# Recurrence levels multiplied as 32x32 diagonal blocks in one core's hybrid decoder layer

## The chip, the cores and the metric

The kernel runs on one core of a Trainium2 chip. The metric is the device time of one execution in microseconds (us), lower being better. Matrix products run on TensorE (PE in the profile; its weight loads are PEld), elementwise work on VectorE (DVE), ScalarE (ACT) and GpSimd (POOL), and transfers are issued mostly from SyncE (SP).

## The reference

One decoder layer over 16 learned tokens ("meta") and 2048 sequence tokens of width 1024. An input projection feeds three token mixers; their outputs are joined, projected, normalised, and go through a gated MLP. The change is inside the second mixer, a gated linear recurrence of four heads of width 128, which the reference computes chunk by chunk:

```python
G = jnp.cumsum(gb, axis=2)                              # gb: log of the forget gate
diff = G[:, :, :, None, :] - G[:, :, None, :, :]
decay = jnp.where(mask, jnp.exp(jnp.where(mask, diff, 0.0)), 0.0)   # lower triangle
A = jnp.einsum('bhtd,bhsd,bhtsd->bhts', qb, kb, decay)
o_intra = jnp.einsum('bhts,bhse->bhte', A, ib)
```

Every pair of tokens s <= t has its own vector of decays, so A is not one product of two matrices.

## The kernel before

The sequence goes through the mixers in four blocks of 512 tokens (`NB`, `TB`), each held as four tiles of 128 tokens (`TT`, `P`). Block 0 also carries the 16 meta tokens. For each block `Mixers.run` is a generator that issues the big projections: `cols_proj` and `rows_proj` multiply activations by weights through `mm3` (L117 to L119), three products per operand pair, since each operand is split in a rounded part and a remainder (`split`, L112 on ACT and L113 on DVE, into `w_hi` and `w_lo`, three buffers of each).

For each block and head, `Mixers.head` builds the 128x128 matrix A of each of the four tiles by levels of doubling. At the level of run length w, tokens are paired in runs of w; the products of all keys of an even run with all queries of the odd run next to it can be written with one common reference point, and so become a matrix product. `level(w, ka, qa)` does this for w = 1 (before the loop over `LEVELS`; its mask also takes the diagonal) and, in the loop, for w = 2, 4, 8 and 16: 5 calls per head, 80 in all. Each call multiplies the whole 128x128 tile (L402, four matmuls into one bank), and one masked copy on DVE (L403, `copy_predicated`, 128x512) takes the valid entries into A. In block 0, calls with w < 16 (4 per head, 16 in all) also do the 16x16 matrix of the meta tokens (L407, L408). For w = 32 and 64, `level_wide` multiplies only the blocks that are needed (L415: eight matmuls with 32 weight columns for w = 32, in partitions 0-31 and 64-95 in turn; four with 64 for w = 64) and copies these blocks into A (L419). POOL and DVE prepare the operands of each level (L427, L428, L430, L431). At the end of the head A is the weight operand of L486.

The masks are built once at the start by `level_masks` on POOL: five 128x128 tiles, each with a buffer of its own.

What sets the order: `drive` interleaves the generators, one step of a head after each step of the projections; PE keeps exactly the order in which the program issues its instructions (`manual_schedule`), while the other engines' queues are ordered by a scheduler ahead of the run, from priorities (weight loads and splits are raised by `AHEAD`) and its own model of times.

Of the kernel before, what the change touches and what calls it, by code (L numbers as in the profile page):

```python
# [10 lines left out]
F32 = mybir.dt.float32  # L11
F32R = mybir.dt.float32r
U32 = mybir.dt.uint32
# [5 lines left out]
P = 128  # L19
# [7 lines left out]
TT = TB // P  # L27
# [5 lines left out]
T_CB, T_CC, T_CV, T_Q, T_F, T_PV = 0, 2, 4, 6, 10, 14  # L33
POOL_WINDOWS = (2, 4, 8, 16)
LEVELS = (2, 4, 8, 16, 32, 64)
ALPHA = 2.0 ** 0.25
LN_EPS = 1e-5
RMS_EPS = 1e-6
# [16 lines left out]
def bcast_rows(row, n):  # L55

    return bass.AP(row.tensor, row.offset, [[0, n], row.ap[-1]])


class Common:  # L60
# [38 lines left out]
    def bank(self):  # L99
        return self.ps.tile([P, 512], F32, tag="bank", name="bank")  # L100
# [115 lines left out]
class Mixers:  # L216
# [5 lines left out]
    def __init__(self, ctx, cm, lower, w_feat, w_rows, w_conv, w_pool, pool_scale, norm_g, w_o, x, xT, meta,  # L222
                 metaT, ln1, x1):
        self.cm, self.nc = cm, cm.nc
        nc, tc = cm.nc, cm.tc
        self.x, self.xT, self.meta, self.metaT, self.ln1, self.x1 = x, xT, meta, metaT, ln1, x1
        self.key_eng = nc.gpsimd
        self.pooled = []
        self.w_feat, self.w_rows, self.w_o = w_feat, w_rows, w_o
        cpool = ctx.enter_context(tc.tile_pool(name="m_const", bufs=1))  # L230
        self.ipool = ctx.enter_context(tc.tile_pool(name="m_i", bufs=5))
        self.hpool = ctx.enter_context(tc.tile_pool(name="m_h", bufs=1))

        self.ng = cpool.tile([P, P], F32, name="ng")
        nc.gpsimd.dma_start(self.ng, bcast_rows(norm_g, P))
        self.ctaps = cpool.tile([P, 2, 3], F32, name="ctaps")
        nc.gpsimd.dma_start(self.ctaps, w_conv)
        self.pscale = cpool.tile([P, 2], F32, name="pscale")
        nc.gpsimd.dma_start(self.pscale, pool_scale)
        self.wp = cpool.tile([P, 2, P], F32, name="wp")  # L240
        nc.vector.memset(self.wp, 0.0)
        for m in range(2):
            for h in range(2):
                nc.gpsimd.dma_start(self.wp[h * 64:(h + 1) * 64, m, h * 64:(h + 1) * 64], w_pool[2 * m + h])
        self.lower_bounds(cpool, lower)
        self.level_masks(cpool)


        self.cnt = cpool.tile([P, 2, NM], F32, name="cnt")
        for m in range(2):  # L250
            nc.gpsimd.iota(self.cnt[:, m, :], pattern=[[1, NM]], base=1, channel_multiplier=0,
                           allow_small_or_imprecise_dtypes=True)
            for h in range(2):
                hs = slice(h * 64, (h + 1) * 64)
                nc.vector.tensor_scalar_min(self.cnt[hs, m, :], self.cnt[hs, m, :],
                                            float(POOL_WINDOWS[2 * m + h]))
        nc.vector.reciprocal(self.cnt, self.cnt)


        self.a_buf = [cpool.tile([P, TT, P], F32, name=f"a{i}") for i in range(2)]  # L260
        self.a_meta = cpool.tile([NM, NM], F32, name="a_meta")
        for t in self.a_buf + [self.a_meta]:
            nc.vector.memset(t, 0.0)

        self.inv = cpool.tile([P, WC], F32, name="inv")
        nc.vector.memset(self.inv, 1.0)
        self.state = [cpool.tile([P, P], F32, name=f"state{h}") for h in range(NH)]
        self.chalo = [cpool.tile([P, 2], F32, name=f"chalo{m}") for m in range(2)]
        self.phalo = [cpool.tile([P, NM], F32, name=f"phalo{m}") for m in range(2)]
# [23 lines left out]
    def level_masks(self, pool):  # L293

        nc = self.nc
        self.masks = {}
        for h in (1, 2, 4, 8, 16):
            mk = pool.tile([P, P], F32, name=f"mask{h}")
            nc.gpsimd.memset(mk, 1.0)
            a = P // (2 * h)  # L300
            if h > 1:

                v = mk.rearrange("p (a u s) -> p a u s", u=2, s=h)
                nc.gpsimd.memset(v[:, :, 0, :], 0.0)
                t, pat = v[:, :, 1, :], [[1, a], [0, h]]
                tests = [(ALU.is_ge, 0, -2 * h, 1), (ALU.is_gt, h, 2 * h, -1)]
                for op, base, step, sign in tests:
                    nc.gpsimd.affine_select(out=t, in_=t, compare_op=op, fill=0.0, base=base,
                                            pattern=[[step, a], [0, h]], channel_multiplier=sign)
            else:  # L310

                v = mk.rearrange("p (a u) -> p a u", u=2)
                tests = [(0, ALU.is_equal, 0, -2, 1), (1, ALU.is_ge, 0, -2, 1), (1, ALU.is_ge, 1, 2, -1)]
                for u, op, base, step, sign in tests:
                    nc.gpsimd.affine_select(out=v[:, :, u], in_=v[:, :, u], compare_op=op, fill=0.0, base=base,
                                            pattern=[[step, a]], channel_multiplier=sign)
            self.masks[h] = mk.bitcast(U32)

    def row_tiles(self, b):
        return [(NM + t * P, P) for t in range(TT)] + ([(0, NM)] if b == 0 else [])  # L320
# [51 lines left out]
    def head(self, b, h, q, k, pre, vals, gates, sums, outs):  # L372
# [6 lines left out]
        nc, cm, s, bank = self.nc, self.cm, self.span(b), self.cm.bank  # L379
        mm = nc.tensor.matmul  # L380

        def runs(t, w, sl):
            return t[:, sl].rearrange("p (a u s) -> p a u s", u=2, s=w)
# [9 lines left out]
        nc.vector.tensor_mul(prep[:, :, 1, :], prep[:, :, 1, :], prep[:, :, 0, :])  # L393
        yield 2

        A, Am = self.a_buf[h % 2], self.a_meta
        main = [NM + t * P for t in range(TT)]

        def level(w, ka, qa):
            pt = bank()  # L400
            for t, c in enumerate(main):
                mm(pt[:, t * P:(t + 1) * P], lhsT=ka[:, c:c + P], rhs=qa[:, c:c + P], start=True, stop=True)  # L402
            nc.vector.copy_predicated(A, self.masks[w].unsqueeze(1).to_broadcast([P, TT, P]),  # L403
                                      pt.rearrange("p (t c) -> p t c", t=TT))
            if b == 0 and w < NM:
                pm = bank()
                mm(pm[0:NM, 0:NM], lhsT=ka[:, 0:NM], rhs=qa[:, 0:NM], start=True, stop=True)  # L407
                nc.vector.copy_predicated(Am, self.masks[w][0:NM, 0:NM], pm[0:NM, 0:NM])  # L408

        def level_wide(w, M):  # L410
            pt = bank()
            starts = range(0, P, 2 * w)
            for t, c in enumerate(main):
                for o in starts:
                    mm(pt[o:o + w, t * P + o + w:t * P + o + 2 * w],  # L415
                       lhsT=M[:, c + o:c + o + w], rhs=M[:, c + o + w:c + o + 2 * w], start=True, stop=True)
            ptv = pt.rearrange("p (t c) -> p t c", t=TT)
            for o in starts:
                nc.vector.tensor_copy(A[o:o + w, :, o + w:o + 2 * w], ptv[o:o + w, :, o + w:o + 2 * w])  # L419

        level(1, kB, qB)
        for w in LEVELS:
            sl = slice(0 if b == 0 and w < NM else NM, WC)
            M = self.wide("work", WORK)
            Mv, kv, qv, prev, postv = (runs(t, w, sl) for t in (M, k, q, pre, post))
            end = [P, prev.shape[1], w]
            self.key_eng.tensor_mul(Mv[:, :, 0, :], kv[:, :, 0, :], postv[:, :, 0, :])  # L427
            self.key_eng.tensor_mul(postv[:, :, 0, :], postv[:, :, 0, :],  # L428
                                    prev[:, :, 1, w - 1:w].to_broadcast(end))
            nc.vector.tensor_mul(Mv[:, :, 1, :], qv[:, :, 1, :], prev[:, :, 1, :])  # L430
            nc.vector.tensor_mul(prev[:, :, 1, :], prev[:, :, 1, :], prev[:, :, 0, w - 1:w].to_broadcast(end))  # L431
            yield 1
            if w < 32:
                level(w, M, M)
            else:
                level_wide(w, M)
        qG, kG = self.wide("work", WORK), self.wide("work", WORK)
        self.key_eng.tensor_mul(kG[:, s], k[:, s], post[:, s])
        nc.vector.tensor_mul(qG[:, NM:], q[:, NM:], pre[:, NM:])
# [11 lines left out]
        pt = bank()  # L451
# [136 lines left out]
    def out_proj(self, b, half, res):  # L588
# [11 lines left out]
        for (u, c, n), r in zip(prod, res):  # L600
            nc.vector.scalar_tensor_tensor(r[0:n, nn], in0=r[0:n, nn], scalar=ALPHA, in1=u[0:n],
                                           op0=ALU.mult, op1=ALU.add)
# [86 lines left out]
class Ffn:  # L689
# [357 lines left out]
    def down(self, b):  # L1047
# [4 lines left out]
        for t in range(2 * nu):  # L1052
            r = self.dpool.tile([P, D], F32, tag="row", name="row", bufs=2 * nu + 2)
            t0 = b * UT + t * P
            nc.sync.dma_start(r, self.x1[NM + t0:NM + t0 + P, :])
            nc.scalar.mul(r, r, ALPHA)
            rows.append(r)
# [175 lines left out]
```

## Time and profile before

| | us |
|---|---|
| median of 3 runs | 2333.89 (2333.07 to 2335.82) |
| the profiled execution, its own time | 2332.45 |
| its span, first to last instruction | 2330.7 |
| PE busy in the span | 2249.5 (97%) |
| DVE busy | 1673.3 (72%) |
| ACT busy | 890.6 (38%) |
| POOL busy | 860.0 (37%) |
| mean granted TensorE clock | 0.988 of full speed |

The head work lies between about 50 and 881 us; the rest of the span is the MLP, which has no levels. A busy engine is one with an instruction in flight; matmuls overlap in the pipeline, so what one of them costs is read from the distance between starts, not from its duration. One fp32 matmul leaves two records in the trace (320 matmuls on L402 are 640 records), one in the rounded format of L117 to L119 leaves one.

### The profile page before, as it was taken

The numbers are of one execution on the slowest core, as the hardware profiler recorded it, in microseconds if no ns is written. First come the engines' busy times: TensorE is split into PE (matmuls) and PEld (weight loads), VectorE is DVE, ScalarE is ACT, GpSimd is POOL, SyncE is SP. The second block draws the span as 40 slices with busy tenths as digits, with TensorE's granted clock in tenths as the row PEclk, the third lists the DMA queues.
The fourth block names the chain that finished last, engine by engine and source line by source line (L and its number), as shares of the span: only waits on it lengthen the run. The fifth ranks groups of instructions, "written<-read, shape, count | busy, mean of one in ns | idle before, by whom it ended". The sixth has DMA issues, their size and how long they took to land.

```text
span 2330.7 us, 33935 instructions
## 1 busy us (share of the span) xinstructions
PE 2249.5 (97%) x12692; PEld 1923.7 (83%) x12692; DVE 1673.3 (72%) x2277; ACT 890.6 (38%) x1400; POOL 860.0 (37%) x872
## 2 busy tenths in 40 slices
PE   8999999999999999999998997999999999999996
PEld 6898878788878877899998997788888887887775
DVE  4676777777857697887787777777777756475658
ACT  3233322332343235344443445444444454344332
POOL 3442433143315236354367443444444414000400
PEclk9999999999999999999999998999999999999998
DMA  6222222422452254555566436566666586567553
GB/s 211 67 71 92 73 68 88 159 82 71 149 183 73 82 166 153 207 187 189 191 199 243 145 146 216 187 190 203 196 197 195 189 299 222 195 236 244 181 183 133
DMA packets 182536, 382.25 MB, mean 164 GB/s; under 512 B 16722, under 2 KB 78370, under 8 KB 182372
## 3 DMA queue, kind: packets, MB, share of 16 engines
q1 hardware_dynamic: 166692, 336.66, 43.6%
q10 hardware_dynamic: 14496, 40.06, 4.7%
q0 software_dynamic: 1184, 3.37, 0.4%
q8 instruction: 99, 1.62, 0.3%
q14 instruction: 65, 0.53, 0.1%
HBM read 275.63 MB, written 104.41 MB: 163 GB/s over the span
## 4 chain that ended last, share of the span: by engine, by line
PE 80%; DVE 7%; POOL 4%; DMA 4%; issue 3%; ACT 1%; SPq 0%; DVEq 0%; ACTq 0%; POOLq 0%
PE bank L895 32%; PE bank L1044 14%; PE bank L117 9%; PE bank L118 9%; PE bank L119 9%; PE bank L402 3%; DVE w_lo L113 2%; POOL pw L563 1%; ACT w_hi L112 1%; DMA row<-x 1%; DVE row L210 1%; PE bank L415 1%; PE bank L676 1%; DVE row L959 1%; PE bank L485 1%
## 5 line engine op out<-in xcount | busy, mean ns | idle before, releaser
L113 DVE TENSOR_TENSOR w_lo<-raw,w_hi 128x512 fp32r<-128x512 f32 (+1 forms) x467 | 483.4, 1052 | 289.0 <-ACT w_hi L112 282.1
L112 ACT CAST w_hi<-raw 128x512 fp32r<-128x512 f32 (+1 forms) x467 | 359.6, 787 | 794.8 <-PE bank L119 257.1
L1044 PE MATMUL bank<-w_hi,w_lo 128*128 128x512 f32 x616 | 242.3, 393 | 9.7 <-DVE w_lo L113 9.6
L1044 PE MATMUL bank<-w_hi 128*128 128x512 f32 x616 | 240.9, 391 | 4.1 <-ACT w_hi L112 4.1
L959 DVE SCALAR_TENSOR_TENSOR row<-row,f_taps 128x1024 f32<-128x1024 f32 x176 | 237.0, 1348 | 9.6 <-ACT row L956 4.5
L1044 PE MATMUL bank<-w_lo,w_hi 128*128 128x512 f32 x616 | 240.6, 391 | 0.0
L117 PE MATMUL bank<-xhi,w_hi 128*128 128x512 f32 (+1 forms) x640 | 235.5, 368 | 0.0
L119 PE MATMUL bank<-xhi,w_lo 128*128 128x512 f32 (+1 forms) x640 | 226.0, 353 | 0.1
L118 PE MATMUL bank<-xlo,w_hi 128*128 128x512 f32 (+1 forms) x640 | 226.0, 353 | 0.0
L112 ACT CAST w_hi<-s 128x1024 fp32r<-128x1024 f32 x88 | 92.4, 1051 | 310.6 <-PE bank L895 203.0
L113 DVE TENSOR_TENSOR w_lo<-s,w_hi 128x1024 fp32r<-128x1024 f32 x88 | 124.2, 1412 | 75.0 <-ACT w_hi L112 74.2
L1044 PEld LDWEIGHTS bank<-w_hi,w_lo 128*128 128x128 f32 x616 | 116.0, 188 | 40.0 <-DVE w_lo L113 16.2
L956 ACT ACTIVATE row<-row,f_bias,f_taps 128x1024 f32<-128x1024 f32 x88 | 109.6, 1246 | 78.7 <-DVE row L950 74.9
L1044 PEld LDWEIGHTS bank<-w_hi 128*128 128x128 f32 x616 | 116.2, 189 | 28.1 <-ACT w_hi L112 4.6
L1077 POOL TENSOR_TENSOR row<-row,du 128x512 f32<-128x512 f32 x24 | 47.6, 2017 | 248.3 <-DVE du L1075 246.5
L1044 PEld LDWEIGHTS bank<-w_lo,w_hi 128*128 128x128 f32 x616 | 116.1, 189 | 25.0
L119 PEld LDWEIGHTS bank<-xhi,w_lo 128*128 128x128 f32 x640 | 121.0, 189 | 17.7 <-DVE w_lo L113 0.5
L117 PEld LDWEIGHTS bank<-xhi,w_hi 128*128 128x128 f32 x640 | 121.2, 189 | 16.6 <-ACT chi L112 0.5
L118 PEld LDWEIGHTS bank<-xlo,w_hi 128*128 128x128 f32 x640 | 121.4, 190 | 15.2 <-issue 0.7
L117 PE MATMUL bank<-w_hi,xhi 128*128 128x512 f32 x272 | 112.9, 415 | 7.6 <-ACT xhi L112 7.6
L428 POOL TENSOR_TENSOR work<-work,pre 128x256 f32<-128x256 f32 (+1 forms) x96 | 88.1, 917 | 82.0 <-DVE pre L431 61.5
L117 PE MATMUL bank<-w_hi,chi 128*128 128x512 f32 x272 | 112.1, 412 | 2.8 <-ACT w_hi L112 2.8
(293 smaller groups left out, 5601.2 us busy)
## 6 DMA issues: line engine op xcount, KB each, us to landing
raw<-a_ops SPq DMA_DIRECT2D x70, 512.0 KB, 4.6
raw<-in_w_up_dram SPq DMA_DIRECT2D x66, 512.0 KB, 4.9
raw<-in_w_feat_dram SPq DMA_DIRECT2D x64, 512.0 KB, 3.3
s_up<-s SPq DMA_DIRECT2D x44, 512.0 KB, 2.7
a_ops<-a_t SPq DMA_DIRECT2D x88, 256.0 KB, 2.1
s<-s_up SPq DMA_DIRECT2D x44, 512.0 KB, 5.2
raw<-s_down SPq DMA_DIRECT2D x40, 512.0 KB, 3.6
a_ops<-row SPq DMA_DIRECT2D x66, 256.0 KB, 2.5
```

The lines of the kernel that those rows point to most:

```text
L112: self.nc.scalar.copy(hi, src)
L113: self.nc.vector.tensor_sub(lo, src, hi.bitcast(F32))
L117: mm(out, lhsT=a_hi, rhs=b_hi, start=first, stop=False)
L118: mm(out, lhsT=a_hi, rhs=b_lo, start=False, stop=False)
L119: mm(out, lhsT=a_lo, rhs=b_hi, start=False, stop=last)
L402: mm(pt[:, t * P:(t + 1) * P], lhsT=ka[:, c:c + P], rhs=qa[:, c:c + P], start=True, stop=True)
L428: self.key_eng.tensor_mul(postv[:, :, 0, :], postv[:, :, 0, :], prev[:, :, 1, w - 1:w].to_broadcast(end))
L895: mm(u[:, 0:n], lhsT=wp[:, kc], rhs=xp[o][k][:, at:at + n], start=start, stop=k == 3 and i == 2, skip_group_check=True)
L956: nc.scalar.activation(y, c[:, 2:UT + 2], AF.Identity, bias=self.bias[:, i:i + 1], scale=self.taps[:, i, 2:3])
L959: nc.vector.scalar_tensor_tensor(y, in0=c[:, d:UT + d], scalar=self.taps[:, i, d:d + 1], in1=y, op0=ALU.mult, op1=ALU.add)
L1044: mm(bank, lhsT=x, rhs=y, start=first and k == 0 and i == 0, stop=k == HK - 1 and i == 2, skip_group_check=True)
L1077: nc.gpsimd.tensor_add(rows[t][:, f], rows[t][:, f], us[u])
```

## The change

`level` multiplies, for each tile, only the four 32x32 blocks on the diagonal: sixteen matmuls with 32 weight columns and 32 moving columns instead of four with 128 and 128. Block o of a tile goes to partitions o to o+31 of the bank, tile t to columns 32t to 32t+31, so the four blocks lie side by side. The masked copy then covers 128x128 elements and goes into a tile of its own, `near` (two of them, taken in turn by heads). After all levels of a head, four ACT copies of 32x(4x32) move `near` into the diagonal blocks of A. The masks become 128x32: each full mask is built in one of two buffers in turn and its four diagonal blocks are copied by ACT.

```diff
+R = 32
-        for t in self.a_buf + [self.a_meta]:
+        self.near = [cpool.tile([P, TT, R], F32, name=f"near{i}") for i in range(2)]
+        for t in self.a_buf + self.near + [self.a_meta]:
             nc.vector.memset(t, 0.0)
...
-            mk = pool.tile([P, P], F32, name=f"mask{h}")
+            mk = pool.tile([P, P], F32, tag="mask", name="mask", bufs=2)
...
-            self.masks[h] = mk.bitcast(U32)
+            near = pool.tile([P, R], F32, name=f"mask{h}")
+            for o in range(0, P, R):
+                nc.scalar.copy(near[o:o + R], mk[o:o + R, o:o + R])
+            self.masks[h] = near.bitcast(U32)
...
-        A, Am = self.a_buf[h % 2], self.a_meta
+        A, Am, near = self.a_buf[h % 2], self.a_meta, self.near[h % 2]
...
             for t, c in enumerate(main):
-                mm(pt[:, t * P:(t + 1) * P], lhsT=ka[:, c:c + P], rhs=qa[:, c:c + P], start=True, stop=True)
-            nc.vector.copy_predicated(A, self.masks[w].unsqueeze(1).to_broadcast([P, TT, P]),
-                                      pt.rearrange("p (t c) -> p t c", t=TT))
+                for o in range(0, P, R):
+                    mm(pt[o:o + R, t * R:(t + 1) * R], lhsT=ka[:, c + o:c + o + R], rhs=qa[:, c + o:c + o + R],
+                       start=True, stop=True)
+            nc.vector.copy_predicated(near, self.masks[w].unsqueeze(1).to_broadcast([P, TT, R]),
+                                      pt[:, 0:TT * R].rearrange("p (t c) -> p t c", t=TT))
...
+        for o in range(0, P, R):
+            nc.scalar.copy(A[o:o + R, :, o:o + R], near[o:o + R])
```

On PE nothing changes place; here is the last `level` call of block 0, head 0, before, between the input projection's matmuls (w_hi, xhi are split operands, work the level's operand).

```order
L117 MATMUL bank<-w_hi,xhi_117 16x512
L118 MATMUL bank<-w_lo,xhi_117 16x512
L119 MATMUL bank<-w_hi,xlo_125 16x512
L402 MATMUL bank<-work 128x128 x4
L117 MATMUL bank<-w_hi,xhi_118 128x512
L118 MATMUL bank<-w_lo,xhi_118 128x512
```

And now, at the same place.

```order
L118 MATMUL bank<-w_hi,xhi_117 16x512
L119 MATMUL bank<-w_lo,xhi_117 16x512
L120 MATMUL bank<-w_hi,xlo_125 16x512
L410 MATMUL bank<-work 32x32 x16
L118 MATMUL bank<-w_hi,xhi_118 128x512
L119 MATMUL bank<-w_lo,xhi_118 128x512
```

The four matmuls became sixteen small ones, and the projection goes on behind them as before. ACT's queue gets new entries; before, at the end of block 0, head 3, it read so (a weight split is a CAST, kT and km belong to the head's next steps).

```order
L176 DMA row<-in_xT_dram 128x1024
L112 CAST w_hi<-raw 128x512 x5
L450 COPY km<-bank 16x128
L455 COPY kT<-bank 128x512
L112 CAST w_hi<-raw 128x512
```

Now the four copies of `near` into A stand between two weight splits.

```order
L177 DMA row<-in_xT_dram 128x1024
L113 CAST w_hi<-raw 128x512 x2
L447 COPY a_223<-near_226 32x4x32 x4
L113 CAST w_hi<-raw 128x512 x3
L461 COPY km<-bank 16x128
L466 COPY kT<-bank 128x512
```

Three weight splits are queued behind the copies there. The other fifteen heads get their four copies at the corresponding place, some with an ACT operation of another part of the block between them.

## Rows read from the trace of the kernel before

**Rows 1.** The page's first line, and one stretch by engine (--windows).

```profile
PE 2249.5 (97%) x12692; PEld 1923.7 (83%) x12692; DVE 1673.3 (72%) x2277; ACT 890.6 (38%) x1400; POOL 860.0 (37%) x872
60.00:870.00 810.00, 801.15 (x4642) 667.61 (x4639) 596.15 (x1032) 263.18 (x571) 284.83 (x290) 1.00 0.31 101
```

**Rows 2.** PE's waits, 0 to 900 us: total us, times, longest.

```profile
PE bank L117 <- ACT xhi L112: 7.6, 1, 7.6
PE bank L485 <- DVE st L468: 6.6, 4, 2.4
```

**Rows 3.** PE's timeline at a level without meta: start, us, operation.

```profile
269.22 0.40 PE L118 MATMUL bank<-w_lo,xhi 128*128 128x512 f32 x1
269.45 0.39 PE L119 MATMUL bank<-w_hi,xlo 128*128 128x512 f32 x1
269.69 1.05 PE L402 MATMUL bank<-work 128*128 128x128 f32 x8
270.50 0.48 PE L117 MATMUL bank<-xhi,w_hi 128*128 128x512 f32 x1
270.81 0.39 PE L118 MATMUL bank<-xlo,w_hi 128*128 128x512 f32 x1
```

**Rows 4.** PE's timeline at a level with meta, block 0.

```profile
70.11 0.39 PE L119 MATMUL bank<-w_hi,xlo 128*16 128x512 f32 x1
70.34 1.05 PE L402 MATMUL bank<-work 128*128 128x128 f32 x8
71.32 0.21 PE L407 MATMUL bank<-work 128*16 128x16 f32 x2
...
71.80 0.40 PE L118 MATMUL bank<-w_lo,xhi 128*128 128x512 f32 x1
```

**Rows 5.** PE's timeline at a w = 32 level (L415).

```profile
284.23 0.39 PE L119 MATMUL bank<-xhi,w_lo 128*128 128x512 f32 x1
284.55 0.45 PE L415 MATMUL bank<-work 128*32 128x32 f32 x16
284.92 0.50 PE L117 MATMUL bank<-w_hi,chi 128*128 128x512 f32 x1
285.26 0.40 PE L118 MATMUL bank<-w_lo,chi 128*128 128x512 f32 x1
```

**Rows 6.** Another w = 32 level, from two later starts: first record left, records left.

```profile
84.34 0.39 PE L415 MATMUL bank<-work 128*32 128x32 f32 x14
...
84.46 0.27 PE L415 MATMUL bank<-work 128*32 128x32 f32 x6
```

**Rows 7.** PE by line and form: records, busy us, mean ns.

```profile
L402 PE MATMUL bank<-work 128*128 128x128 f32 x640 | 84.3, 275 | 0.1
L415 PE MATMUL bank<-work 128*64 128x64 f32 x128 | 10.9, 228 | 0.0
L415 PE MATMUL bank<-work 128*32 128x32 f32 x256 | 7.1, 199 | 0.0
```

**Rows 8.** DVE by line and form: the masked copies.

```profile
L403 DVE COPY_PREDICATED a<-mask,bank 128x512 f32<-128x512 uint32 x80 | 58.3, 728 | 0.1
L408 DVE COPY_PREDICATED a_meta<-mask,bank 16x16 f32<-16x16 uint32 x16 | 2.4, 149 | 0.0
```

**Rows 9.** ACT by line and form: small copies.

```profile
L466 ACT COPY st<-state 128x128 f32<-128x128 f32 x16 | 4.7, 296 | 14.3 <-PE bank L485 8.1 <-DVE state L460 3.9 <-DVE state L468 2.1
L112 ACT CAST xhi<-early 128x16 fp32r<-128x16 f32 x8 | 1.2, 198 | 0.0
```

**Rows 10.** ACT's timeline: an early input split, and one weight split behind head 3's levels.

```profile
24.00 0.62 ACT L112 CAST xhi<-row 128x512 fp32r<-128x512 f32 x1 [2.77 <-DMA row<-in_xT_dram]
...
217.55 0.62 ACT L112 CAST w_hi<-raw 128x512 fp32r<-128x512 f32 x1 [3.02 <-PE bank L119]
```

**Rows 11.** DVE's timeline: head 3's last masked copy.

```profile
215.17 0.73 DVE L403 COPY_PREDICATED a<-mask,bank 128x512 f32<-128x512 uint32 x1
```

**Rows 12.** Ten us around one PE wait for L468, by engine; then clock, DMA.

```profile
605.00:615.00 10.00, 8.05 (x37) 6.58 (x36) 9.99 (x18) 2.67 (x8) 4.87 (x4) 0.83 0.28 105
```

## The prediction

> **What bounds the kernel now.** I read the page's busy times first, then the stretch in which the heads run, then PE's waits there, then PE's timeline at the places that change. PE is busy 97% of the span, and from 60 to 870 us, where the changed work lies, 801 of 810 us; DVE has 596, ACT 263 and POOL 285 us of work in it [rows 1]. A busy PE could still be a waiting one with something in flight, so the second look is at its waits: up to 900 us its two largest are 7.6 us once for the first input and 6.6 us in four places for the state chain on DVE (L468) [rows 2]. At the level sites themselves the projection's matmuls before and behind stand at their ordinary step of 0.23 us [rows 3]. So here PE's queue is the clock of the kernel: what a level takes out of PE's sequence is taken from the end, and what it adds is added.
>
> **PE: what a level costs now.** Durations overlap, so I count from the last projection matmul ahead to the second one behind, and take off the two ordinary steps. Without meta: 269.45 to 270.81 is 1.36, less 2 x 0.233 (the step from 269.22 to 269.45): 0.89 us for four 128x128 matmuls [rows 3]. With meta: 70.11 to 71.80 is 1.69, less 0.47: 1.22 us [rows 4]. There are 80 sites, 16 of them with meta.
>
> **PE: what it will cost.** The kernel already has matmuls of the new shape: at w = 32, eight with 32 weight and 32 moving columns. There 284.23 to 285.26 is 1.03, less 0.47: 0.56 us [rows 5]. Between 84.34 and 84.46, 8 of the 16 records go, which is 4 matmuls in 0.12 us or 0.03 us each [rows 6]; the eight take 0.25 us, and the other 0.31 us is the way into and out of this shape. How fast one such matmul would go alone is bounded by the other shapes: a 128-wide record takes (270.50-269.69)/8 = 0.10 us [rows 3], a quarter of it 0.025; a 64-wide one, which never has a neighbour in other partitions, 10.9/128 = 0.085 us, half of it 0.043 [rows 7]. Two records make a matmul: 0.05 to 0.085 us, and I take 0.06, near the 128-wide rows, where the pipeline is full. At w = 32 one matmul in 0.03 us is thus two running side by side, those that write partitions 0-31 and 64-95.
>
> The new site has sixteen, in four groups of partitions in turn. If all four groups run side by side, sixteen take four rounds of 0.06, 0.25 us, as the eight in two groups do now, and the site costs 0.56 and about 0.02 for starting the further groups: 0.58 us. Saved without meta: 0.89 - 0.58 = 0.31 us, times 64 is 19.8 us. The meta matmul has 16 weight columns; now it adds 1.22 - 0.89 = 0.33 us behind a 128-wide one [rows 3, 4]. Behind 32-wide ones it lies between 0.06 (two records, each alone at 0.03) and that 0.33. I take 0.10, nearer to the low end, because the cost at w = 32 was mostly the change of shape and here the shape was changed already. Saved: 1.22 - 0.68 = 0.54 us, times 16 is 8.6 us (4.9 to 9.3 by the bounds). Together 28.4 us.
>
> The rows show the way in: L415 begins 0.32 us behind the last ordinary start, 0.09 later than usual [rows 5]. The Trainium skill, "TensorEngine Tiling (Array Packing)", Key Properties, says that changing the tiling mode drains the engine, and that tiles load weights and multiply independently, four of them with 128 rows and 32 columns. By that rule each site pays the drain once and four groups run at once, which is the 0.58 above; the trace agrees for two groups, and no row here shows four. Another page speaks against the change: "TensorE: Matmul & The Clock Gate", Wait — 56ns, not 53.3ns?, says start-to-start never falls below about 25 ns. Taken for records, 32 of them would need 0.80 us (estimate), 1.11 with the 0.31, slower than now; rows 6 have eight in 0.12 us, 15 ns each, so it does not hold in that form. Taken for whole matmuls it is not refuted, and is the first rival.
>
> **DVE.** The masked copy shrinks from 512 to 128 columns. It takes 728 ns with 512 and 149 ns with 16 columns [rows 8]; on the line between them 128 columns are 149 + 112 x 579/496 = 280 ns. 80 x 0.45 = 36 us of DVE work go. I count nothing for them, since PE and not DVE sets the pace, but per head DVE is relieved of 2.2 us while PE runs 1.6 (5 x 0.31) to 2.5 us faster (0.31 + 4 x 0.54), so DVE does not become the late engine by this change. The bound on this side is the 6.6 us of waits for L468 [rows 2] and the halved clock behind some of them: around one, PE lost 1.95 us idle and the mean clock of the 10 us was 0.83, some 1.7 us more [rows 12]. If all that went, the gain would be up to 10 us larger; the scheduler has also put masked copies ahead of weight splits and moved normalisation work at block ends, which may cost as much. I take zero. Two extra zero fills lie in DVE's idle time at the start.
>
> **ACT.** It gets 64 copies of 32x(4x32). The nearest rows are 296 ns for 128x128 and 198 ns for 128x16 [rows 9]: 64 x 0.2 to 0.3 = 13 to 19 us on an engine that is busy 263 of 810 us [rows 1]. What is behind them matters: weight splits, for which PE waits in the end. Head 3 as example: its last masked copy ends at 215.17 + 0.73 = 215.90 [rows 11]; the next split, which cannot start before PE frees a buffer, starts at 217.55 after 3.02 us of idling [rows 10]. The four copies, at most 1.2 us, fit in these 1.65 us. Without this cover a split would be late by up to 1.2 us, and PE would wait only if it had eaten the two other buffers, 24 matmuls of 0.233 or 5.6 us of its work. A is read by L486 well after the head's levels, so the new wait of PE on ACT there is met early.
>
> At the start 20 mask copies of at most 0.2 us, 4 us, come between the input splits, and POOL's third and later masks wait for ACT's copies, since there are two buffers. ACT idles 2.77 us before 24.00 for a DMA [rows 10]. The split started there feeds the seventh of eight steps of 15 matmuls: 7.6 + 6 x 15 x 0.233 = 28.6 us at the earliest [rows 2, 3], 4 us later. Masks are needed only from 50 us on. Nothing is counted.
>
> **The sum.** 2332.45 - 28.4 = 2304.0 us for the profiled execution. The median of the runs before is 1.4 us above its profiled execution; so 2305.5 us.
>
> **The rivals.**
>
> *Two at a time.* Nothing in the trace has more than two groups of partitions in flight, and the 0.03 us per matmul at w = 32 [rows 6] is as well explained by a fixed spacing of matmuls. Then sixteen take 0.50, the site 0.81 us: 0.08 x 64 = 5.1 and, with meta at 0.91, 0.31 x 16 = 5.0; gain 10.1, 2324 us. For it: exactly 0.03 for every one. Against: records come in pairs, so the spacing inside a pair is well below that.
>
> *Neighbouring groups exclude each other.* At w = 32 the two groups are 0-31 and 64-95; the new order goes 0, 32, 64, 96, and 64-wide matmuls occupy two neighbours as one. If neighbours can't overlap, each matmul takes 0.06: 1.0 us, 1.31 with the 0.31. That is 0.42 x 64 = 27 us more without meta and (1.41 - 1.22) x 16 = 3 us more with: 2364 us. A site gets slower from 0.036 us per matmul on, (0.89 - 0.31)/16. Against it: nothing in the rows says that place matters.
>
> *Given back at the block ends.* PE arrives earlier where DVE is full (9.99 of 10 us [rows 12]), the four waits for L468 grow, or splits are held up by the copies of A. Doubling the 6.6 us and the clock loss behind them costs 10 us, and 16 heads x 0.3 us a further 5: 2320 us. Against: DVE is relieved more than PE.
>
> *The change does not do what it says* only if the small matmuls lower the granted clock. One stretch like that of rows 12 costs 1.7 us, so it would take one in every head to undo the sum; after w = 32 and 64, which have been there all along, the clock's mean is 1.00 over the 810 us [rows 1]. I put that into the third.
>
> **How the numbers follow.** Four groups at once 0.66 (2298 to 2312 with meta's bounds and some of the DVE waits either way), two at a time 0.18, given back 0.09, neighbours exclude each other 0.07. About 0.2%, 4.7 us, can be told from no change. Faster takes the first two and most of the third, 0.89; within 0.2% 0.05; slower the last and a little of the third, 0.06. The range goes from 2297 to 2326, which takes in two at a time.
>
> **What would show it.** PE's timeline at a level site: 32 records, and 0.37 to 0.40 us from the first start to the next projection matmul where it is 0.81 now; 0.62 would be two at a time, 1.1 or more the exclusion. L403's successor at about 0.28 us. PE's waits for L468 no longer than before, none on a split that stands behind the copies of A. The forecast is wrong if PE's sequence between the sites has new gaps, above all at the block ends as in [rows 12], or if the sites shorten and the end does not move by 80 times as much.

## The result and the profile after

The changed kernel takes 2302.6 us (median of 4 runs, 2299.5 to 2328.4), the kernel before, run beside it, 2333.5 (4 runs): a ratio of 0.9882, interval 0.9847 to 0.9916. Some executions of either kernel come out 10 to 37 us longer than the rest, so the intervals are wide, and below I go by medians and by what the profiled executions show place by place. The profiled execution took 2304.4 us, its span is 2302.7 (before 2330.7): 28.0 us less.

The page's first line, and one stretch by engine (columns as in [rows 1]; the stretch ends 28 us earlier, as the heads now do):

```profile
PE 2219.7 (96%) x14612; PEld 1873.7 (81%) x14612; DVE 1641.5 (71%) x2279; ACT 914.0 (40%) x1484; POOL 852.7 (37%) x872
60.00:842.00 782.00, 771.02 (x6562) 616.11 (x6561) 568.81 (x1031) 282.79 (x636) 280.63 (x289) 1.00 0.34 106
```

PE has 1920 more records and 30 us less busy time, DVE 32 us less, ACT 23 us more. PE is still busy for all but 11 us of the stretch, so its queue is still the clock of the kernel. The mean granted clock of the stretch reads 1.00 as before: the small matmuls did not lower it.

PE's timeline at a level without meta, answering [rows 3]:

```profile
260.85 0.40 PE L120 MATMUL bank<-xhi,w_lo 128*128 128x512 f32 x1
261.18 0.46 PE L410 MATMUL bank<-work 128*32 128x32 f32 x32
261.57 0.50 PE L118 MATMUL bank<-xhi,w_hi 128*128 128x512 f32 x1
261.91 0.39 PE L119 MATMUL bank<-xlo,w_hi 128*128 128x512 f32 x1
```

The 32 records begin 0.33 us behind the last projection matmul, and the next projection matmul 0.39 behind them, where it was 0.81. Counted as the prediction counts, 261.91 - 260.85 less two steps of 0.233 is 0.59 us; over the 53 such sites with nothing else in them it is 0.585 to 0.59.

At a level with meta, answering [rows 4]:

```profile
68.72 0.39 PE L120 MATMUL bank<-w_hi,xlo 128*16 128x512 f32 x1
69.03 0.46 PE L410 MATMUL bank<-work 128*32 128x32 f32 x32
69.31 0.20 PE L416 MATMUL bank<-work 128*16 128x16 f32 x2
...
69.78 0.40 PE L119 MATMUL bank<-w_lo,xhi 128*128 128x512 f32 x1
```

This is 1.06 - 0.47 = 0.59 us again (median of the sixteen 0.607): the meta matmul adds some 0.02 us where it added 0.33.

The same kind of site seen from two later starts, as in [rows 6] (records left at each):

```profile
77.31 0.41 PE L410 MATMUL bank<-work 128*32 128x32 f32 x28
...
77.43 0.28 PE L410 MATMUL bank<-work 128*32 128x32 f32 x12
```

16 records, 8 matmuls, go in 0.12 us, which is 0.015 us per matmul; with two groups it was 0.03.

The line that replaces the first of [rows 8], on DVE, and the two that ACT got (records, busy us, mean ns, then idle time before them and what ended it):

```profile
L412 DVE COPY_PREDICATED near<-mask,bank 128x128 f32<-128x128 uint32 x80 | 23.6, 295 | 52.9 <-PE bank L410 46.2 <-PE bank L416 6.6
L447 ACT COPY a<-near 32x128 f32<-32x128 f32 x64 | 19.0, 296 | 9.4 <-DVE near L412 7.2 <-issue 0.4
L323 ACT COPY mask<-mask 32x32 f32<-32x32 f32 x20 | 4.3, 214 | 0.9 <-POOL mask L311 0.7
```

PE's waits up to 960 us (total us, times, longest), answering [rows 2]:

```profile
PE bank L118 <- ACT xhi L113: 7.6, 1, 7.6
PE bank L119 <- DVE w_lo L114: 6.3, 5, 2.7
PE bank L496 <- DVE st L479: 4.1, 3, 2.0
...
PE bank L687 <- DMA row<-x: 2.9, 1, 2.9
...
PE bank L410 <- DVE work L439: 1.1, 1, 1.1
```

The waits for the state chain fell from 6.6 to 4.1 us. Four others are new or longer: a row of x that has not landed (2.9), level operands on DVE (1.1 and 0.6), and the split remainders (5.1 before, 6.3 now).

Where the time shows up at the end is read from the first matmuls of the MLP. The line of one up-projection matmul (min, median and max ns, then first and last start), before and after:

```profile
L895 PE MATMUL bank<-xt2h,w_hi x264: 281/286/398, 959.0 to 1857.9; 128*128 128x258 f32 x88, 128*128 128x512 f32 x44
```

```profile
L906 PE MATMUL bank<-xt2h,w_hi x264: 281/286/398, 931.5 to 1831.8; 128*128 128x258 f32 x88, 128*128 128x512 f32 x44
```

27.5 us of the 28.0 are there when the MLP begins, all gained ahead of it. The sites give 64 x (0.89 - 0.585) + 16 x (1.22 - 0.607) = 29.3 us; PE's idle time ahead of the MLP went from 24.3 to 27.6 us, 3.3 more. That leaves 26.0 against 27.5; the other 1.5 us I did not trace. The granted clock does not account for it: half of PE's busy time at the lower clock level, summed over the stretches ahead of the MLP, is 6.8 us before and 6.7 after.

### The profile page after: what moved, and what is told of

Same layout as the page of the kernel before. It is cut to its first block, busy times and chain, and to the rows that moved or that the text cites. A ratio compares the mean times of both kernels' runs of the same rounds, so it can differ in the third digit from the quotient of the medians.

```text
span 2302.7 us, 37840 instructions
## 1 busy us (share of the span) xinstructions
PE 2219.7 (96%) x14612; PEld 1873.7 (81%) x14612; DVE 1641.5 (71%) x2279; ACT 914.0 (40%) x1484; POOL 852.7 (37%) x872
## 4 chain that ended last, share of the span: by engine, by line
PE 79%; DVE 8%; POOL 4%; DMA 4%; issue 3%; ACT 1%; SPq 0%; DVEq 0%; POOLq 0%; ACTq 0%
PE bank L906 33%; PE bank L1055 14%; PE bank L118 10%; PE bank L119 9%; PE bank L120 9%; DVE w_lo L114 3%; PE bank L410 1%; DVE row L213 1%; DVE row L211 1%; DMA piece<-x1T 1%; PE bank L424 1%; POOL pw L574 1%; ACT w_hi L113 1%; PE bank L687 1%; DMA row<-x 1%
## 5 line engine op out<-in xcount | busy, mean ns | idle before, releaser
L113 ACT CAST w_hi<-raw 128x512 fp32r<-128x512 f32 (+1 forms) x467 | 359.7, 787 | 762.3 <-PE bank L120 235.9
L114 DVE TENSOR_TENSOR w_lo<-raw,w_hi 128x512 fp32r<-128x512 f32 (+1 forms) x467 | 481.1, 1046 | 230.1 <-ACT w_hi L113 221.8
L113 ACT CAST w_hi<-s 128x1024 fp32r<-128x1024 f32 x88 | 92.4, 1051 | 312.9 <-PE bank L906 205.3
L114 DVE TENSOR_TENSOR w_lo<-s,w_hi 128x1024 fp32r<-128x1024 f32 x88 | 123.2, 1401 | 77.2 <-ACT w_hi L113 76.8
L119 PE MATMUL bank<-w_lo,chi 128*128 128x512 f32 x272 | 108.9, 400 | 6.3 <-DVE w_lo L114 6.3
```

The source lines that it names most:

```text
L113: self.nc.scalar.copy(hi, src)
L114: self.nc.vector.tensor_sub(lo, src, hi.bitcast(F32))
L119: mm(out, lhsT=a_hi, rhs=b_lo, start=False, stop=False)
```

## The experiments

Three theories were tested: the level sites carry the gain because all four groups of partitions run at once; DVE's 35 us of relief and the copies of A on ACT are worth little; a wait further on takes back whatever PE gains beyond that. Each kernel is an edit of the changed one, shown as a diff against it.

**The changed kernel once more**, on the chip on which the doubled copy, the copies on DVE and the joined levels (below) ran; the other experiments ran on other chips.

> The changed kernel itself, unaltered, to be measured beside the other kernels: 2300 to 2304 us, 29 to 33 us below the kernel before, if its earlier runs stand for it. One of its four earlier executions took 2328; if such executions come with this kernel and not with the kernel before, about one in four of these is again near 2328.

2306.6 us (6 runs, 2304.3 to 2341.3) against 2334.0: 0.9875 (0.9832 to 0.9917), as in the first comparison, though above the 2300 to 2304 us that were expected: medians of one and the same kernel differ by 4 us. Its MLP begins 0.1 us from that of the profile above, its span is 1.4 us longer, and the spans of this kernel's single executions lie mostly between 2297.8 and 2305.6 us. So a difference of 2 to 4 us between two spans says little; the begin of the MLP is the steadier mark.

**The order of the sixteen matmuls, by groups.**

```diff
-            for t, c in enumerate(main):
-                for o in range(0, P, R):
+            for o in range(0, P, R):
+                for t, c in enumerate(main):
                     mm(pt[o:o + R, t * R:(t + 1) * R], ...
```

> The same sixteen matmuls per level, but the four that write one group of partitions follow one another (groups outside, tiles inside). Theory (a matmul runs beside its neighbours in the queue only if they write other groups; alone it takes 0.06 us): 16 x 0.0625 = 1.0 us and 0.31 for the shape, 1.31 per site where the changed kernel has 0.58: 0.73 x 80 = 58 us slower than the changed kernel, about 2361, slower than before too. Rival (small matmuls follow at a fixed spacing whatever their group, or the queue picks matmuls of other groups from further back): as the changed kernel, 2300 to 2306.

2333.5 us (10 runs, 2329.0 to 2337.7), 0.9961 (0.9922 to 1.0001) of before: the whole gain is gone with the same matmuls, copies and masks in the program. PE's timeline at the level w = 16 of block 0, which has no meta:

```profile
78.47 0.39 PE L120 MATMUL bank<-w_hi,xlo 128*16 128x512 f32 x1
78.79 0.90 PE L410 MATMUL bank<-work 128*32 128x32 f32 x32
...
79.96 0.39 PE L119 MATMUL bank<-w_lo,xhi 128*128 128x512 f32 x1
```

1.49 - 0.47 = 1.02 us. The direction is the theory's, the size is not: I had matmuls of one group follow one another at 0.06 and so a site of 1.31. Seen from later starts in the same site:

```profile
78.88 0.81 PE L410 MATMUL bank<-work 128*32 128x32 f32 x30
...
79.16 0.54 PE L410 MATMUL bank<-work 128*32 128x32 f32 x16
```

14 records in 0.28 us are 20 ns each, against 7.5 in the order by tiles. The experiment after the next says what one alone takes. Such a site costs even more than the 0.89 us of the four 128x128 matmuls; that the time is level with before all the same comes from the shorter sites with meta and, as the run with the 128x128 matmuls suggests, from DVE's lighter work.

**Two groups at a time**, partitions 0 and 32 through the four tiles, then 64 and 96.

```diff
-            for t, c in enumerate(main):
-                for o in range(0, P, R):
-                    mm(...)
+            for pair in ((0, R), (2 * R, 3 * R)):
+                for t, c in enumerate(main):
+                    for o in pair:
+                        mm(...)
```

> The same sixteen matmuls per level, with the groups 0-31 and 32-63 taking turns through all tiles, then 64-95 and 96-127. Theory (as many run at once as there are groups in turn): 0.50 us for the sixteen, 0.81 to 0.83 per site: 0.24 x 80 = 19 us slower than the changed kernel, about 2322. Rival (neighbouring groups exclude each other): 1.31 per site, about 2361. Rival (fixed spacing): 2300 to 2306.

2311.4 us (4 runs, 2309.9 to 2313.9), 0.9885 (0.9839 to 0.9931); its span is 2312.2, 8 to 9.5 us above the two of the unaltered kernel, and its MLP begins at 936.7 us, 5.2 later. None of the expected times (2322, 2361, 2300 to 2306) was met. The site:

```profile
76.80 0.39 PE L120 MATMUL bank<-w_hi,xlo 128*16 128x512 f32 x1
77.12 0.60 PE L411 MATMUL bank<-work 128*32 128x32 f32 x32
...
77.99 0.39 PE L119 MATMUL bank<-w_lo,xhi 128*128 128x512 f32 x1
```

1.19 - 0.47 = 0.72 us, 0.13 above the order by tiles, so the first rival's state (two groups in flight) is really slower than what the changed kernel has; but again less than the 0.81 of the sum.

**One group only**: all sixteen matmuls write partitions 0 to 31. Their number, shape and operands stay; three quarters of the diagonal blocks of A are left empty.

```diff
-                    mm(pt[o:o + R, t * R:(t + 1) * R], ...)
-            nc.vector.copy_predicated(near, ...)
+                    mm(pt[0:R, t * R + 4 * o:t * R + 4 * o + R], ...)
+            nc.vector.copy_predicated(near[0:R], ...)
```

> The sixteen matmuls of a level all write partitions 0-31 (columns 512 of the bank), and only those partitions of near are filled, so three quarters of the diagonal blocks of A are left empty. Theory (alone in its group one such matmul takes 0.06 us, two records of 0.031; groups issued one after another overlapped because the queue starts matmuls of the next group early): 16 x 0.0625 = 1.0 us, 1.3 per site, some 58 us slower than the changed kernel. Rival (what slows one group after another is not the group but something shared, so that one group alone costs as little as that did): about 1.03 per site and 2333 us.

2359.8 us (one run), 53 to 57 above the unaltered kernel, as the theory had it. The site, and two later looks into it:

```profile
79.95 0.39 PE L120 MATMUL bank<-w_hi,xlo 128*16 128x512 f32 x1
80.27 1.20 PE L410 MATMUL bank<-work 128*32 128x32 f32 x32
...
81.74 0.39 PE L119 MATMUL bank<-w_lo,xhi 128*128 128x512 f32 x1
```

```profile
80.32 1.15 PE L410 MATMUL bank<-work 128*32 128x32 f32 x31
...
80.83 0.64 PE L410 MATMUL bank<-work 128*32 128x32 f32 x15
```

1.79 - 0.47 = 1.32 us, and 16 records in 0.51 us: 32 ns each, 0.063 us per matmul where nothing runs beside it. That is the 0.06 which the prediction took between 0.05 and 0.085. So the changed kernel's 0.015 per matmul is four side by side, and 0.03 at w = 32 was two. With 0.063 the two sites before can be told better: if matmuls begin in program order, and one waits only for the one ahead in its own group, the order by groups has three waits of 0.063 in each of four groups and one more at the end, 0.82 us where the order by tiles has 0.25, a site of 0.585 + 0.57 = 1.15; by pairs 0.45, a site of 0.785. Measured are 1.02 and 0.72, less by 0.13 with three changes of group and by 0.06 with one. What saves the further 0.04 to 0.06 at each change these runs do not settle. The Trainium skill, "TensorE: Matmul & The Clock Gate", The mechanism, says that a weight load for a row group that is not in conflict, or for the background weight buffer, is pulled ahead of matmuls in flight, while the matmuls keep their order. The groups here differ in output partitions and share all 128 rows, so this would fit at most by the background buffer; no run here takes that apart.

**The 128x128 matmuls back, the small masked copy kept** (it takes the first 128 columns, so A is not the reference's; only what DVE and ACT do is that of the changed kernel).

```diff
-                for o in range(0, P, R):
-                    mm(pt[o:o + R, t * R:(t + 1) * R], ...)
+                mm(pt[:, t * P:(t + 1) * P], lhsT=ka[:, c:c + P], rhs=qa[:, c:c + P], ...)
```

> The matmuls of a level are again four of 128x128, and the masked copy takes its 128x128 elements from the first 128 columns of the bank (the values of the first tile for all four, so the matrix A is not the right one); near, the masks and the copies on ACT as in the changed kernel. Theory (the whole gain is PE's): within 4 us of the kernel before, 2329 to 2337, although DVE has 35 us less to do. Rival (the smaller masked copy on DVE brings a good part): 10 us or more below the kernel before.

2330.0 us (10 runs, 2328.1 to 2366.4), 0.9949 (0.9908 to 0.9989), within the theory's 2329 to 2337; its span is 2327.5, 3.2 below the one before. So 35 us less of DVE work, with ACT's copies added and the queues ordered anew, is worth about 3 us at the end, not nothing. Ahead of the MLP it is worth more: its line of the up-projection starts 5.4 us earlier than before.

```profile
L904 PE MATMUL bank<-xt2h,w_hi x264: 280/286/398, 953.6 to 1855.0; 128*128 128x258 f32 x88, 128*128 128x512 f32 x44
```

PE's waits up to 960 us:

```profile
PE bank L685 <- DMA row<-x: 4.7, 3, 2.9
...
PE bank L494 <- DVE st L477: 1.7, 3, 1.4
```

The state waits fall from 6.6 to 1.7, and a wait for x comes up in their place even though no site has become shorter. PE's idle time is therefore only about 1 us less; what goes is the lower clock. Before, the granted clock fell to its lower level behind two state waits of 1.94 and 1.95 us ([rows 12] has one); here those two waits are gone, and up to 900 us the clock does not fall at all, 3.5 us less lost ahead of the MLP. From here to the changed kernel the small matmuls bring 23.4 to 24.8 us of span, 4.5 to 6 less than the 29.3 at the sites; at the begin of the MLP it is 22.1, 7.2 less.

**The masked copy twice**: the reverse, 24 us of DVE work added.

```diff
-            nc.vector.copy_predicated(near, ...)
+            for _ in range(2):
+                nc.vector.copy_predicated(near, ...)
```

> Each masked copy of near is done twice, 80 x 0.295 = 24 us more of DVE work, nothing else. Theory (PE's sequence sets the end while the heads run and DVE has room): within 4 us of the changed kernel, 2299 to 2307. Rival (DVE sets the end in much of the stretch, and its relief was a good part of the gain): 10 to 24 us slower than the changed kernel.

2315.0 us (7 runs, 2313.3 to 2316.4), 0.9907 (0.9878 to 0.9936): 8 to 12 us slower than unaltered, and the expectation of at most 4 fell. The 160 copies keep DVE busy for 47.3 us. The largest of PE's new waits:

```profile
PE bank L410 <- DVE work L440: 6.2, 1, 6.2
```

It lies at 394 us, at the end of a block. DVE's timeline ahead of it (start, us, operation):

```profile
391.35 0.28 DVE L413 COPY_PREDICATED near<-mask,bank 128x128 f32<-128x128 uint32 x1
391.55 0.67 DVE L534 TENSOR_TENSOR cp<-cp,bank 128x512 f32<-128x512 f32 x1
...
392.94 1.26 DVE L213 SCALAR_TENSOR_TENSOR row<-row,ln_rs,ln_b 128x1024 f32<-128x1024 f32 x1
```

Between these rows DVE has no gap, and the normalisation of the block before and the convolution stand between a level's copy and the next level's operands. Behind the wait the granted clock falls to its lower level (columns as in [rows 1]; the unaltered kernel reads 1.00 in the same ten microseconds):

```profile
396.00:406.00 10.00, 5.74 (x42) 4.01 (x43) 9.42 (x17) 1.48 (x3) 5.62 (x5) 0.51 0.76 272
```

The MLP begins 6.7 us later than in the unaltered kernel. The wait of 6.2 and the loss of clock behind it (half of the 5.74 us busy, 2.9) come to 9.1; where 2.4 of them are won back I did not trace. The remaining 3 to 4 us of the span come inside the MLP and I have no cause for them.

**The copies of A on DVE** instead of ACT.

```diff
-            nc.scalar.copy(A[o:o + R, :, o:o + R], near[o:o + R])
+            nc.vector.tensor_copy(A[o:o + R, :, o:o + R], near[o:o + R])
```

> The 64 copies of near into A go to DVE instead of ACT: ACT loses 19 us, DVE gains about 64 x 0.28 = 18 us. Theory (both are hidden beside PE): within 4 us of the changed kernel. Rival (the copies on ACT hold up weight splits and so give back part of the gain): 4 us or more faster than the changed kernel, and fewer PE waits for weight splits (L113, L114).

2308.3 us (4 runs, 2307.8 to 2309.9), 0.9878 (0.9833 to 0.9923); 2 us above the control by the median, 4 by the span. It is not faster, and PE's waits for splits up to 960 us are those of the changed kernel (6.3 us for L114, 2.7 for L113), so the copies on ACT do not hold up the splits. What else ACT's relief may bring is not shown, since DVE got 17 us of work for it.

**Two levels side by side**: level 1 is held back and issued with level 2, 4 with 8, 16 with 32, so that PE changes its shape four times per head instead of seven. If the saving at the sites could be added on, this should give it.

```diff
-        level(1, kB, qB)
+        held = (1, kB, qB)
...
             yield 1
+            if held is None and w < 64:
+                held = (w, M, M)
+                continue
+            if held is not None:
+                level(*held)
+                held = None
```

> The matmuls of level 1 are held back and issued right ahead of those of level 2, those of 4 ahead of 8, and of 16 ahead of 32: three sites fewer per head. Theory (each site pays about 0.31 us for the way into and out of the small shape, whatever is in it): 3 x 16 x 0.31 = 15 us less than the changed kernel, about 2288 us, and two levels back to back in PE's sequence with no gap. Rival (the later issue of half the levels makes the masked copies bunch on DVE and PE wait for operands or banks): 2298 or more, with new waits of PE at these sites.

2304.7 us (6 runs, 2302.7 to 2306.8), 0.9864 (0.9824 to 0.9903). A site for two levels, and PE's waits up to 960 us:

```profile
255.83 0.39 PE L120 MATMUL bank<-w_hi,xlo 128*128 128x512 f32 x1
256.15 0.76 PE L410 MATMUL bank<-work 128*32 128x32 f32 x64
...
257.18 0.39 PE L119 MATMUL bank<-xlo,w_hi 128*128 128x512 f32 x1
```

```profile
PE bank L119 <- DVE w_lo L114: 8.2, 7, 2.1
...
PE bank L502 <- DVE st L485: 6.7, 4, 2.0
PE bank L693 <- DMA row<-x: 6.0, 3, 3.0
```

1.35 - 0.47 = 0.88 us for two levels that take 2 x 0.585 = 1.17 apart: at the sites the saving is there, some 14 us in all. But PE's idle time ahead of the MLP is 36.6 us instead of 27.6 (30.3 in the control), the MLP begins 6.1 us earlier, and the span is 2 to 3.4 us shorter. So past this point a gain on PE is turned into waits for DVE and for x. From the begin of the MLP to the end it then takes 2.6 to 3.9 us longer than the two unaltered executions; PE's idle time there and half of its busy time at the lower clock add up to 70.5 us, against 66.2 and 68.0, which is that loss. What starts it stays open.

The runs so far, put side by side, show how the gain at the sites and the begin of the MLP go together (one profiled execution each, sites by the median of those with nothing else in them, both columns against the kernel before):

| run | sites shorter by, us | MLP earlier by, us |
|---|---|---|
| one group | -30 | -23.3 |
| by groups | -5 | -0.5 |
| 128x128 back | 0 | 5.4 |
| two groups | 18 | 22.3 |
| changed kernel | 29 | 27.5 |
| two levels side by side | 43 | 33.5 |

Up to 18 us at the sites, 4 to 7 us more than the sites save reach the MLP, which fits DVE's relief. At 29 that surplus is gone and 2 us are missing, at 43 it is 10 us that are missing.

**The state chain ahead of everything else on DVE and ACT**, in the changed kernel and on top of the joined levels.

```diff
-        nc.scalar.copy(st[:, 0, :], state)
-        for t in range(TT):
-            nc.vector.scalar_tensor_tensor(...)
+        with cm.tc.high_priority(offset=AHEAD):
+            nc.scalar.copy(st[:, 0, :], state)
+            for t in range(TT):
+                nc.vector.scalar_tensor_tensor(...)
```

> The changed kernel with the state chain of each head (its copy on ACT and the four operations on DVE that L496 of the changed kernel waits for) raised in the scheduler's priorities, so that no long normalisation operation stands between its steps. Theory (at the block ends PE waits for this chain behind normalisation work, 4.1 us, and the halved clock behind two of the waits costs about 3.4 more): those waits go, 5 to 8 us less than the changed kernel, 2296 to 2300. Rival (what is moved back makes other things late: weight splits, the rows of the normalisation and the transposes behind them): within 3 us of the changed kernel, with as much waiting elsewhere.

> The merged levels (1 with 2, 4 with 8, 16 with 32) together with the raised state chain. Theory (merging saves 14 us at the sites, but 9 us of new waits at block ends, above all for the state chain, took most of it): with the chain raised about 2294, the best of all. Rival (the waits move to splits and to the transposes' rows): 2300 or more.

Alone 2303.4 us (6 runs, 2300.0 to 2305.5), 0.9812 (0.9751 to 0.9873) of a kernel before whose median was 2354.4 us in that comparison; against 2302.6 and 2306.6 for the unaltered kernel it is no difference. With the joined levels 2306.5 us (6 runs, 2303.7 to 2335.3), 0.9863 (0.9794 to 0.9932). The begin of the MLP alone, then the largest of PE's waits with the joined levels:

```profile
L907 PE MATMUL bank<-xt2h,w_hi x264: 281/286/398, 927.8 to 1830.7; 128*128 128x258 f32 x88, 128*128 128x512 f32 x44
```

```profile
PE bank L694 <- DMA row<-x: 10.5, 4, 4.9
```

Alone, the wait for the state is gone (0.2 us), PE idles 2 to 5 us less ahead of the MLP, and the MLP begins 3.7 us earlier; from there to the end it takes 3 to 4 us longer. So the theory holds in part up to the MLP, where 5 to 8 us were expected, and at the end nothing of it can be told from the spread of single executions. With the joined levels the state wait is 2.0 us, the rows of x are waited for instead (10.5), and the MLP begins 5.0 us later than with the joined levels alone (930.5 against 925.5): there the expectation's rival holds. None of these versions is clearly better than the changed kernel: unaltered and altered they all lie between 2302 and 2307 us.

## Why the prediction was right, point by point

- *PE's queue is the clock of the kernel.* Right, up to a limit: of 29.3 us at the sites, and 5.4 of DVE's relief, 27.5 reached the MLP. The joined levels show the limit: 14 us more at the sites became 6 at the MLP and 2 to 3 at the end.
- *0.58 us for a site without meta.* Right: 0.585 to 0.59, in four groups at once. The 0.06 us for one matmul alone and the 0.31 for the way in and out were both right; the run with one group gives 0.063, and 1.32 - 16 x 0.063 = 0.31.
- *0.10 us for the meta matmul.* Mis-sized: 0.02, below the low end of 0.06. Saved 9.8 us instead of 8.6. It writes partitions 0 to 15, and the runs agree with a wait for that group only: it adds 0.04 us where all sixteen wrote there (one group), 0.02 here, and nothing measurable in the order by groups, where that group was done first.
- *280 ns for the masked copy.* 295 ns. The straight line between two sizes of [rows 8] was 5% low.
- *DVE's relief counted at nothing.* The weakest step, though within its bounds: the run with the 128x128 matmuls puts it at 5.4 us ahead of the MLP and about 3 us of span, and the doubled copy shows that the other direction costs 8 to 12. The reason given, that PE and not DVE sets the pace, is true of the average and not of the block ends. After the change the place of [rows 12] looks as it did, with DVE full, the wait, and the fall of the clock behind it:

```profile
580.00:590.00 10.00, 8.04 (x37) 6.56 (x35) 9.99 (x17) 2.36 (x8) 5.08 (x5) 0.83 0.30 106
```

  What DVE runs ahead of the state link that PE wanted:

```profile
581.28 0.34 DVE L479 SCALAR_TENSOR_TENSOR st<-st,pre,bank 128x128 f32<-128x128 f32 x1
...
581.63 1.80 DVE L211 SCALAR_TENSOR_TENSOR row<-row,ln_mv,ln_g 128x1024 f32<-128x1024 f32 x1
583.36 1.21 DVE L114 TENSOR_TENSOR w_lo<-raw,w_hi 128x512 fp32r<-128x512 f32 x1
584.49 0.33 DVE L479 SCALAR_TENSOR_TENSOR st<-st,pre,bank 128x128 f32<-128x128 f32 x1
```

- *ACT's copies are covered.* Right. 296 ns each, the upper of the two rows in [rows 9], although they have 32 partitions; 19.0 us, the upper end of 13 to 19. Head 3, the example: the four copies run from 203.27 to 204.49, and the next split starts at 205.96 after idling, for a buffer that PE frees:

```profile
203.27 1.22 ACT L447 COPY a<-near 32x128 f32<-32x128 f32 x4
205.96 0.62 ACT L113 CAST w_hi<-raw 128x512 fp32r<-128x512 f32 x1 [1.47 <-PE bank L120]
```

- *The masks cost nothing at the start.* Right: 4.3 us on ACT, and PE's first wait is 7.6 as before.
- *Given back at the block ends.* A rival by its chance, yet part of it came: between the 128x128 matmuls and the small ones the begin of the MLP moves by 7.2 us less than the sites, the span by 4.5 to 6 less. The prediction's own sign of being wrong, new gaps in PE's sequence, is there too: 2.9 us for x, 1.1 and 0.6 for level operands. That the sum of 28.4 met a span 28.0 shorter is partly luck, two errors that cancel: 3 to 5 us of relief not counted, and 5 to 7 us taken back by new waits, with 1 us too little for meta. The forecast time, 2305.5 us, lies between the medians 2302.6 and 2306.6.
- *Two at a time* and *neighbours exclude each other.* Both refuted: 16 records in 0.12 us, and 0.72 and 1.32 us where fewer groups are in flight. The second rival's price for a site, 1.31 us, does occur, but not because groups are neighbours: it is what one group alone costs (1.32). What decides is the order; taking the same groups one after the other costs 27 us.
- *The chances.* One slip: slower got 0.06, although it was to hold the last rival, 0.07, and more.

## What to carry to other kernels

Small matmuls with few weight columns pay where they go to different groups of partitions in turn: the order of two nested loops was worth the whole gain here (2306.6 against 2333.5 us). Measure such a site from the last ordinary matmul ahead to the second one behind; the records' durations overlap and say little. Before the next saving on the same engine is added to a sum, look at which waits stand right behind it: here they, and the MLP behind them, took 14 us down to 2 or 3.

## What the hardware showed beyond the expectation

- An fp32 matmul with 32 weight and 32 moving columns takes 0.063 us where the next goes to the same partitions, and 0.015 where four groups take turns: about a quarter. The two orders between them came out 0.06 and 0.13 us per site below what starting in program order gives.
- The way into and out of this shape costs 0.31 us per site between 128x512 matmuls (what is left of 1.32 without 16 x 0.063), more than the sixteen matmuls themselves (0.25).
- An ACT copy of 32x128 takes 296 ns, as long as one of 128x128 [rows 9], and one of 32x32 takes 214: between these shapes the columns set the time and the partitions do not.
